# Cross-attention queries computed features-first, with their rms factor applied in the exponential and pools that wait by tile

## The chip, the cores and the metric

The kernel runs on one core of a Trainium2 chip. The metric is the device time of one execution in microseconds (us), the lower the better. Engines are named as in the profile: PE is TensorE (matmuls and transposes), DVE is VectorE, ACT is ScalarE, POOL is GpSimd, and SP is the engine that issues the DMA transfers here. Each engine takes its instructions in the order in which they stand in its own program; it waits in that order for semaphores of the others.

## The reference

One layer of an encoder, on 1024 tokens of 1024 features in float32. Three steps, each added to its input:

```
h = x + W_out [ FoX(xn) ++ GLA(xn) ]                      xn = rms_norm(x)
h = h + CrossAttn(rms_norm(h), rms_norm(mem))
y = h + W2 relu(W1 rms_norm(h))^2
```

The second step is the one that changes:

```
q = rms_norm((hn @ wq).reshape(B, S, 4, 256), q_norm_g)
k, v = jnp.split(memn @ wkv, 2, axis=-1)      # 256 memory tokens
k = rms_norm(k.reshape(B, M, 4, 256), k_norm_g)
s = jnp.einsum('bshd,bmhd->bhsm', q, k) / math.sqrt(256)
p = jax.nn.softmax(s, axis=-1)
o = jnp.einsum('bhsm,bmhd->bshd', p, v).reshape(B, S, D)
return o @ wo
```

So every query is divided by the root of its mean square over the 256 features of its head, before the product with k. The gains of the two norms can be moved into k, and they are. The rms of h itself cancels in the norm of q, save for the epsilon: h enters unnormalised, and the epsilon is scaled by h's mean square (`hev`).

## The kernel before

**Precision and matmuls.** Each float32 operand is split in two parts, a high one (names ending in h: wh, sh, qh, th, oh) and a low one (wl, sl, ql, tl, ol). A product of two such operands is three matmuls for each block of 128 summed features: high·high (L110), and the two mixed ones (L111, L112), all in `gemm`. Splitting is one copy on ACT and one subtraction on DVE (`evac_split`, L117 and L118; for weights L99 and L100 with a gain, L88 and L93 without).

**Stages.** `mixer_inputs` and `fox` compute the first step's two kinds of attention up to 559 us. `project_out` (559 to 592 us) multiplies with W_out: for each half of 512 tokens and each of eight blocks of 128 features it takes 12 or 6 matmuls, loads a partial sum hr from memory (L851, three buffers), adds both into h (L856), squares the block on ACT (L169, sqT, three buffers) and sums the squares on POOL (L170, acc). At the end of a half, `token_squares` turns the sums by four transposes into mean squares for each token (hv, hev, hr of `consts`). h stands in SBUF features-first: 128 features in the partitions, 1024 tokens along the row. `xattn` is the second step (592 us to about 750), `project_o_first` and `project_o_rest` its output projection, and `mlp` (from 840 us to the end) the third.

**xattn before.** There are eight units: two pairs of heads (n) by four groups of 256 tokens (u). `queries` takes each of a unit's two token tiles (128 tokens): `split_tile` splits h of this tile over all 1024 features (ACT L819, DVE L820, 128x1024 each), 24 matmuls of 128x512 give the queries of two heads tokens-first, `head_rstd` forms the factor r for each token and head (a Square on ACT, L144; a reduction on DVE, L146; small operations on POOL), DVE multiplies by r (L995), four transposes turn the result features-first (L998), and it is split. `attend` takes a unit's queries: per token tile 12 matmuls of 128x256 for the scores, the negative maximum (L1014), two Exps with the maximum as bias (L1020), POOL scales p by the reciprocal sum (L1024), four transposes (L1027) and a split; then the products with v over 256 tokens (128x256 matmuls), whose split results o go to memory (od, L1038). The projection loads them again as oh and ol (`load_o`), when all heads of a half are stored.

**What sets the order.** The code gives each engine's work in one sequence; a scheduler then orders each engine's program by its own model of the times, keeping to the dependencies. Memory is handed out by pools on two stacks, left and right, of one address range: a pool opened where another was closed gets its memory, and its first users wait for the former users. All loads and stores of this stage stand on one queue of SP.

## Time and profile before

| | us |
|---|---|
| time, median of 3 runs | 1452.56 (1452.08 to 1454.16) |
| the profiled execution | 1454.34 |
| its span | 1452.6 |
| 560 to 720 us: PE busy | 160.00 of 160.00 |
| 720 to 760 us: PE busy | 38.73 of 40.00 |
| 820 to 840 us: PE busy | 18.69 of 20.00 |

The span is what the profiler's records cover; the rest of the execution's time, 1.74 us, lies around it. "Busy" adds up the time in which an engine works on an instruction; a PE instruction's length includes its way through the array, so that matmuls overlap, and the distance of two starts tells what one costs. In the rows of the trace, the text in brackets is the idle time just ahead of the instruction and what ended it. "PEclk" or the column behind the engines' busy times is the granted clock of TensorE, 1.00 at full speed.

### The profile page before, as it was taken

Reading aid. Unit: us, or ns where it says so; the run is one execution under the profiler, and the core shown is the slowest. Engines: PE = TensorE matmul, PEld = TensorE weight load, DVE = VectorE, ACT = ScalarE, POOL = GpSimd, SP = SyncE. Lnnn points to the kernel's source line nnn. Section 1 sums busy time; section 2 is a strip of 40 time slices with the busy share of each in tenths; the row PEclk is TensorE's granted clock in tenths of the full one; section 3 lists DMA queues with packets and bytes.
Section 4 is the critical chain, followed back from the end, with each engine's and each line's share of the span. In section 5 each row is a group of like instructions: output and inputs, shape, how many; then the busy total and the mean of one; then the engine's idle time right before and its main releaser. Section 6 shows DMA issues by size and latency. Waiting matters only on the chain.

```text
span 1452.6 us, 19224 instructions
## 1 busy us (share of the span) xinstructions
PE 1427.7 (98%) x7068; PEld 1190.0 (82%) x7068; DVE 948.6 (65%) x1354; ACT 679.9 (47%) x1095; POOL 397.1 (27%) x404
## 2 busy tenths in 40 slices
PE   9999999998999999999999999999999999999998
PEld 7788788887888887888888878887888888888887
DVE  5366732428798776666644895636556968788796
ACT  4444341327678565455542364445546735335230
POOL 3235513312242223521212300000000542333454
PEclk9999999999999999999999999999999999999999
DMA  8435520268677642412474124444445835336353
GB/s 273 128 73 131 138 70 1 73 176 252 203 211 234 188 140 87 132 59 88 150 266 170 51 80 153 174 174 189 174 174 209 322 121 188 131 122 225 119 198 119
DMA packets 121166, 223.94 MB, mean 154 GB/s; under 512 B 8912, under 2 KB 54512, under 8 KB 118512
## 3 DMA queue, kind: packets, MB, share of 16 engines
q1 hardware_dynamic: 119776, 218.25, 46.5%
q10 hardware_dynamic: 1296, 4.46, 1.0%
q8 instruction: 56, 0.92, 0.3%
q14 instruction: 38, 0.31, 0.1%
HBM read 150.59 MB, written 72.09 MB: 153 GB/s over the span
## 4 chain that ended last, share of the span: by engine, by line
PE 71%; issue 16%; DMA 6%; DVE 3%; ACT 2%; POOL 1%; ACTq 0%; SPq 0%; DVEq 0%; POOLq 0%
PE mm L110 13%; PE mm L112 13%; PE mm L111 13%; PE my L111 5%; PE my L112 5%; PE my L110 5%; PE tr L111 2%; PE tr L112 2%; PE tr L110 2%; PE tr L696 2%; PE pv L703 1%; DMA xt<-in_x_dram 1%; DMA raw<-in_w_in_dram 1%; PE pv L704 1%; PE s L656 1%
## 5 line engine op out<-in xcount | busy, mean ns | idle before, releaser
L111 PE MATMUL my<-x,g 128*128 128x512 f32 x464 | 180.6, 389 | 1.3 <-DVE x L1076 1.3
L110 PE MATMUL my<-x,g 128*128 128x512 f32 x464 | 180.6, 390 | 0.4 <-ACT h L1281 0.4
L112 PE MATMUL my<-x,g 128*128 128x512 f32 x464 | 180.5, 389 | 0.0
L111 PE MATMUL mm<-wl,xh 128*128 128x512 f32 x320 | 126.5, 396 | 0.9 <-DVE wl L100 0.8
L110 PE MATMUL mm<-wh,xh 128*128 128x512 f32 x320 | 126.0, 397 | 1.0 <-DVE sq L307 1.0
L112 PE MATMUL mm<-wh,xl 128*128 128x512 f32 x320 | 125.9, 394 | 0.0
L1075 ACT ACTIVATE g<-s 128x1024 fp32r<-128x1024 f32 (+1 forms) x72 | 68.7, 962 | 105.0 <-PE my L112 39.1
L1076 DVE TENSOR_TENSOR g<-raw,g 128x512 fp32r<-128x512 f32 (+3 forms) x72 | 69.2, 964 | 67.6 <-ACT g L1075 67.4
L111 PEld LDWEIGHTS my<-x,g 128*128 128x128 f32 x464 | 87.1, 188 | 19.9 <-DVE x L1076 1.7
L1101 POOL TENSOR_TENSOR s<-raw 128x384 f32<-128x384 f32 (+1 forms) x20 | 25.8, 1291 | 282.7 <-DVE h L1196 213.8
L110 PEld LDWEIGHTS my<-x,g 128*128 128x128 f32 x464 | 87.1, 188 | 18.8 <-ACT h L1281 0.8
L1075 ACT ACTIVATE g<-raw 128x512 fp32r<-128x512 f32 (+3 forms) x72 | 55.5, 773 | 100.3 <-DMA raw<-in_mlp_w_dram 40.1
L112 PEld LDWEIGHTS my<-x,g 128*128 128x128 f32 x464 | 87.1, 188 | 17.9
L667 POOL TENSOR_SCALAR p<-p,rrec 128x128 f32<-128x128 f32 (+3 forms) x64 | 57.9, 907 | 159.2 <-DVE rrec L666 151.9
L1076 DVE TENSOR_TENSOR g<-s,g 128x1024 fp32r<-128x1024 f32 (+1 forms) x72 | 88.2, 1228 | 7.6 <-ACT g L1075 7.5
L1243 DVE TENSOR_TENSOR x<-x 128x1024 fp32r<-128x1024 f32 (+1 forms) x64 | 76.8, 1220 | 17.3 <-ACT x L1242 17.1
L110 PE MATMUL mm<-x,g 128*128 128x512 f32 x220 | 85.8, 390 | 0.0
L112 PE MATMUL mm<-x,g 128*128 128x512 f32 x220 | 85.7, 389 | 0.0
L111 PE MATMUL mm<-x,g 128*128 128x512 f32 x220 | 85.6, 389 | 0.0
L110 PE MATMUL tr<-x,g 128*128 128x512 f32 x212 | 82.5, 389 | 0.0
L111 PE MATMUL tr<-x,g 128*128 128x512 f32 x212 | 82.5, 389 | 0.0
L112 PE MATMUL tr<-x,g 128*128 128x512 f32 x212 | 82.5, 389 | 0.0
(318 smaller groups left out, 3739.2 us busy)
## 6 DMA issues: line engine op xcount, KB each, us to landing
ud<-h SPq DMA_DIRECT2D x32, 768.0 KB, 3.8
x<-ud SPq DMA_DIRECT2D x48, 512.0 KB, 5.3
raw<-in_mlp_w_dram SPq DMA_DIRECT2D x20, 1024.0 KB, 7.4
raw<-in_mlp_w_dram SPq DMA_DIRECT2D x16, 768.0 KB, 6.0
raw<-in_w_in_dram SPq DMA_DIRECT2D x23, 512.0 KB, 5.0
raw<-in_xattn_wkv_dram SPq DMA_DIRECT2D x16, 512.0 KB, 7.4
od<-o SPq DMA_DIRECT2D x32, 256.0 KB, 4.0
ud<-h SPq DMA_DIRECT2D x32, 256.0 KB, 2.8
```

The lines of the kernel that those rows point to most:

```text
L110: mm(ps, lh[k], rh[k], start=start and k == 0, stop=False, **kw)
L111: mm(ps, lh[k], rl[k], start=False, stop=False, **kw)
L112: mm(ps, ll[k], rh[k], start=False, stop=stop and k == n - 1, **kw)
L656: nc.tensor.matmul(ps[:, c], qa[:, ts], ka[:, c], start=True, stop=False)
L667: nc.gpsimd.tensor_scalar(p[:, 0:n], p[:, 0:n], rr, 1.0, ALU.mult, ALU.mult)
L696: nc.tensor.transpose(o, pp[i][:, kb * P:(kb + 1) * P], self.ident)
L703: nc.tensor.matmul(pv, va[:, kb, :], th[:, js], start=kb == 0, stop=False)
L704: nc.tensor.matmul(pv, va[:, kb, :], tl[:, js], start=False, stop=kb == nb - 1)
L1075: self.nc.scalar.activation(hi, src, AF.Copy)
L1076: self.nc.vector.tensor_tensor(lo, src, f(hi), ALU.subtract)
L1101: eng.tensor_tensor(s[:, 0], raw[:, 3], raw[:, 2], ALU.add)
L1243: nc.vector.tensor_tensor(lo, f(lo), f(hi), ALU.subtract)
```

## The change

Three edits in one.

*Queries features-first.* The units are now four: a pair of heads (n) by a half of 512 tokens. `query` multiplies the other way round, the weights' 128 columns by 512 tokens, so that the queries come out features-first and are split at once, unnormalised. h is split by feature blocks of 128x512 (`split`), each serving all of a unit's four `query` calls. Each result is also squared on ACT (sq, L989); POOL adds the two squares of a head (L993), four transposes turn the sum tokens-first (L996), and a reduction and three small POOL operations give r, a factor for each token and head. r enters as the `scale` of the Exp, and the negative maximum is multiplied by r ahead of it. `scores` works per tile of 128 tokens as before, `values` on 512 tokens at once, and each od store carries both parts of 512 tokens.

*Pools that wait by tile.* The pools of xattn and of the output projection, which follow on others' memory, are opened with `reuse_waits="tile"`: a tile's first user waits for the former users of its own bytes, where it waited for those of the whole pool. Their sizes change: six buffers of queries, 12 pairs of split blocks of h, one buffer of k and v.

*Squares of h's second half.* Its sum has memory of its own (`acc1`), and `h1_factors(1)`, once the end of `project_out`, is called behind the second query.

The core of the diff (unchanged parts of the scores, the outer loop's `keep` and the pools of `project_o_rest` are left out):

```diff
-            self.acc = [self.T(xp, [P, 512], F32, f"acc{i}", bufs=1) for i in range(2)]
+            self.acc = [self.T(xp, [P, 512], F32, "acc", bufs=1), self.acc1]
...
+                if half == 0:
+                    self.h1_factors(half)
...
-                    A = self.split_tile(sp, (self.h[:, :, t * P:(t + 1) * P],))
-                    ps = self.T(mmp, [P, 512], F32, "mm")
-                    self.gemm(ps, *A, *Ws[n])
-                    qn = self.T(qnp, [P, 512], F32, "qn")
-                    r = self.head_rstd(ps, qn, 2, self.hev[:, t:t + 1])
-                    nc.vector.tensor_tensor(v2(qn), v2(ps), self.bcast(r, 256), ALU.mult)
-                    tp = self.T(trp, [P, 512], F32, "tr")
-                    for j in range(4):
-                        nc.tensor.transpose(tp[:, j * P:(j + 1) * P], qn[:, j * P:(j + 1) * P], self.ident)
-                    self.evac_split(qh[:, i], ql[:, i], v4(tp))
...
+            sp = self.open(sst, "sp", 12, side="right", **kw)
+            def split(half, ks):
+                out = []
+                for k in ks:
+                    sh = self.T(sp, [P, 512], F32R, "sh")
+                    sl = self.T(sp, [P, 512], F32R, "sl")
+                    self.evac_split(sh, sl, self.h[:, k, half * 512:(half + 1) * 512])
+                    out.append((sh, sl))
+                return out
+            def query(u, W, A, j):
+                ps = self.T(mmp, [P, 512], F32, "mm")
+                c = slice(j * P, (j + 1) * P)
+                self.gemm(ps, *([w[:, c] for w in w_] for w_ in W), *zip(*A))
+                q = self.T(qp, [P, 2, 512], F32R, "q")
+                self.evac_split(q[:, 0], q[:, 1], ps)
+                Q.setdefault(u, []).append(q)
+                sq = self.T(sqp, [P, 512], F32, "sq")
+                nc.scalar.activation(sq, ps, AF.Square)
+                if j % 2 == 0:
+                    self.sq0 = sq
+                    return
+                nc.gpsimd.tensor_tensor(sq, sq, self.sq0, ALU.add)
+                tp = self.T(trp, [P, 512], F32, "tr")
+                for t in range(4):
+                    nc.tensor.transpose(tp[:, t * P:(t + 1) * P], sq[:, t * P:(t + 1) * P], self.ident)
+                ss = self.T(self.smallp, [P, 4], F32, "ss4")
+                nc.vector.tensor_reduce(ss, v4(tp), AX.X, ALU.add)
+                nc.gpsimd.tensor_scalar(ss, ss, 1.0 / 256, None, ALU.mult)
...
+                nc.gpsimd.tensor_tensor(ss, ss, self.hev[:, 4 * half:4 * half + 4], ALU.add)
...
+                nc.gpsimd.tensor_tensor(R[u][:, j // 2, :], ss, self.mhalf[:, 0:4], ALU.pow)
...
+                nc.vector.tensor_tensor(nm, nm, r, ALU.mult)
...
-                        nc.scalar.activation(p[:, c], ps[:, c], AF.Exp, bias=nm[:, h:h + 1], accum_out=rs[:, h:h + 1])
+                    nc.scalar.activation(p[:, c], ps[:, c], AF.Exp, bias=nm[:, h:h + 1], scale=r[:, h:h + 1], accum_out=rs[:, h:h + 1])
...
+            def values(u):
+                for j in range(4):
+                    pv = self.T(pvp, [P, 512], F32, "pv")
+                    self.gemm(pv, *([vm[:, i, m, c] for m in range(2)] for i in range(2)),
+                              [th[:, m] for m in ms], [tl[:, m] for m in ms])
+                    o = self.T(pp, [P, 2, 512], F32R, "o")
+                    self.evac_split(o[:, 0], o[:, 1], pv)
+                    nc.sync.dma_start(self.od[:, :, half, 4 * n + j, :], f(o))
...
+            units = [(0, 0), (0, 1), (1, 1), (1, 0)]
...
             sst.close()
-            attend(*units[-1], q[-1])
-            self.project_o_first()
+            self.ost, self.O = ExitStack(), {}
+            self.load_o(self.open(self.ost, "op0", side="right", **kw), 1)
+            self.Wo = self.wsplit(self.wo[:, 0:512], None)
+            for t in range(4):
+                scores(3, t)
+            for i in range(4):
+                if i == 2:
+                    values(3)
+                self.o_block(self.Wo, 0, 1, i, self.T(self.mmp, [P, 512], F32, "mm"))
```

Two places in the engines' orders follow. The names carry a running number, which is not the same before and after; a row gives line, operation, output, inputs and shape.

The first place is the passage from `project_out` to the queries, on ACT. Before, the first two token tiles (sh, 128x1024) are split right behind the squares of the first half's blocks, the other tiles later:

```order
L169 ACTIVATE sqT_5983<-h_5805 128x512
L819 ACTIVATE sh_6226<-h_5805 128x1024
L819 ACTIVATE sh_6271<-h_5805 128x1024
L166 ACTIVATE acc_1376_5813<-h_5805 128x512
L169 ACTIVATE sqT_6045<-h_5805 128x512
L99 ACTIVATE wh_6196<-raw_6190,cols_74 128x512
```

and the last squares of the second half stand there, with the third tile behind them:

```order
L169 ACTIVATE sqT_6109<-h_5805 128x512
L99 ACTIVATE wh_6216<-raw_6210,cols_74 128x512
L99 ACTIVATE wh_6888<-raw_6886,cols_74 128x512
L169 ACTIVATE sqT_6122<-h_5805 128x512
L169 ACTIVATE sqT_6135<-h_5805 128x512
L819 ACTIVATE sh_6318<-h_5805 128x1024
```

Now the first split of all stands behind the last square (the wh rows are the queries' weights):

```order
L169 ACTIVATE sqT_6099<-h_5805 128x512
L169 ACTIVATE sqT_6112<-h_5805 128x512
L99 ACTIVATE wh_6206<-raw_6200,cols_74 128x512
L99 ACTIVATE wh_6746<-raw_6744,cols_74 128x512
L169 ACTIVATE sqT_6125<-h_5805 128x512
L169 ACTIVATE sqT_6138<-h_5805 128x512
L117 ACTIVATE sh_6214<-h_5805 128x512
L117 ACTIVATE sh_6218<-h_5805 128x512
```

What was ahead of the second half's squares, the first operands of the queries, is now behind them. On DVE the low parts stand in the same way behind the last additions into h (L843) and two weights' low parts:

```order
L843 TENSOR_TENSOR h_5805<-mm_6104,hr_6102 128x512
L843 TENSOR_TENSOR h_5805<-mm_6117,hr_6115 128x512
L843 TENSOR_TENSOR h_5805<-mm_6130,hr_6128 128x512
L100 SCALAR_TENSOR_TENSOR wl_6207<-raw_6200,cols_74,wh_6206 128x512
L100 SCALAR_TENSOR_TENSOR wl_6747<-raw_6744,cols_74,wh_6746 128x512
L118 TENSOR_TENSOR sl_6215<-h_5805,sh_6214 128x512
L118 TENSOR_TENSOR sl_6219<-h_5805,sh_6218 128x512
```

The second place is the end of the queries, on ACT. Before, the conversions g of the MLP's first weights stand among the queries of the second pair of heads:

```order
L1020 ACTIVATE p_7230,rs_1687_7231<-s_7215,nm_1685_7228 128x256 x2
L117 ACTIVATE o_7097<-pv_7084 128x512
L117 ACTIVATE o_7115<-pv_7102 128x512
L1020 ACTIVATE p_7260,rs_1693_7261<-s_7245,nm_1691_7258 128x256 x2
L1075 ACTIVATE g_1882_8379<-raw_1881_8377 128x512
L117 ACTIVATE qh_7121<-tr_7206 128x512
L117 ACTIVATE th_7213<-tr_7238 128x512
L819 ACTIVATE sh_7503<-h_5805 128x1024
L144 ACTIVATE qn_7342<-mm_7317 128x512
L1075 ACTIVATE g_1884_8384<-raw_1883_8382 128x512
```

Now they stand among the last unit's work, ahead of the Exps of its last two tiles (p, the rows of L1026; o is an output of `values`, th the transposed p):

```order
L117 ACTIVATE o_7379<-pv_7372 128x512
L88 ACTIVATE wh_7824<-raw_7822 128x512
L117 ACTIVATE o_7390<-pv_7383 128x512
L1026 ACTIVATE p_7518,rs_1747_7519<-s_7502,nm_1745_7515,rq_7267 128x256 x2
L1026 ACTIVATE p_7549,rs_1753_7550<-s_7533,nm_1751_7546,rq_7267 128x256 x2
L1106 ACTIVATE g_1845_8202<-raw_1844_8200 128x512
L1106 ACTIVATE g_1847_8207<-raw_1846_8205 128x512
L117 ACTIVATE th_7500<-tr_7526 128x4x128
L1026 ACTIVATE p_7580,rs_1759_7581<-s_7564,nm_1757_7577,rq_7267 128x256 x2
L117 ACTIVATE th_7500<-tr_7557 128x4x128
L117 ACTIVATE o_7401<-pv_7394 128x512
L1026 ACTIVATE p_7611,rs_1765_7612<-s_7595,nm_1763_7608,rq_7267 128x256 x2
```

On SP, the loads of these weights moved with them, to a place behind the first four loads of oh and ol and ahead of the stores od of the third unit:

```order
L80 DMA raw_7480<-in_xattn_wo_dram 128x2x512
L80 DMA raw_7490<-in_xattn_wo_dram 128x2x512
L861 DMA oh_7450<-od_64 128x1024
L862 DMA ol_7451<-od_64 128x1024
L861 DMA oh_7450<-od_64 128x1024
L862 DMA ol_7451<-od_64 128x1024
L80 DMA raw_7822<-in_xattn_wo_dram 128x2x512
L1127 DMA raw_1844_8200<-in_mlp_w_dram 128x2048
L1127 DMA raw_1846_8205<-in_mlp_w_dram 128x2048
L80 DMA raw_7832<-in_xattn_wo_dram 128x2x512
L1047 DMA od_64<-o_7368 256x1x512
L1047 DMA od_64<-o_7379 256x1x512
```

Before, they stood ahead of all oh and ol, among the stores of the fourth unit and ahead of those of the fifth:

```order
L1038 DMA od_64<-o_7097 128x2x256
L1096 DMA raw_1881_8377<-in_mlp_w_dram 128x2048
L1038 DMA od_64<-o_7097 128x2x256
L1038 DMA od_64<-o_7115 128x2x256 x2
L1096 DMA raw_1883_8382<-in_mlp_w_dram 128x2048
L1038 DMA od_64<-o_7288 128x2x256
L1038 DMA od_64<-o_7306 128x2x256
L1038 DMA od_64<-o_7288 128x2x256
L1038 DMA od_64<-o_7306 128x2x256
L80 DMA raw_7823<-in_xattn_wo_dram 128x2x512
L80 DMA raw_7833<-in_xattn_wo_dram 128x2x512
L868 DMA oh_7793<-od_64 128x1024
```

More of the change, by code (lines that the diff above doesn't have):

```diff
@@ L910, in project_o_rest @@
             self.ost.close()
-            self.acc = [self.T(p, [P, 512], F32, "acc") for p in (self.open(mx, "acc", side="right"), xp)]
+            self.acc = [self.acc1, self.T(xp, [P, 512], F32, "acc")]
             x0 = self.open(mx, "x0", 2, side="right", **kw)
@@ L1041, in xattn @@
-            units = [(0, u) for u in range(4)] + [(1, u) for u in (2, 3, 0, 1)]
-            q = []
-            for i, (n, u) in enumerate(units):
-                if i % 4 == 0:
-                    weights(n)
-                q.append(queries(n, u))
-                if i >= 1:
-                    attend(*units[i - 1], q[i - 1])
-                if i == 4:
-                    kst.close()
-            sst.close()
-            attend(*units[-1], q[-1])
-            self.project_o_first()
+            def split(half, ks):
[6 more added lines that the diff above has]
+                return out
@@ new lines, in scores @@
+            def scores(u, t):
+                kT = KV[units[u][0]][0]
+                ts = slice(t * P, (t + 1) * P)
+                if t == 0:
+                    TH[u] = [self.T(ptp, [P, 4, 512], F32R, n) for n in ("th", "tl")]
+                ps = self.T(sps, [P, 512], F32, "s")
+                for h in range(2):
+                    ks = (2 * h, 2 * h + 1)
+                    self.gemm(ps[:, h * M:(h + 1) * M], *([Q[u][k][:, i, ts] for k in ks] for i in range(2)),
+                              *([kT[:, i, k, :] for k in ks] for i in range(2)))
+                r = R[u][:, :, t]
+                nm = self.T(self.smallp, [P, 2], F32, "nm2")
+                nc.vector.tensor_reduce(nm, v2(ps), AX.X, ALU.max, negate=True)
+                nc.vector.tensor_tensor(nm, nm, r, ALU.mult)
+                p = self.T(pp, [P, 512], F32, "p")
+                rs = self.T(self.smallp, [P, 2], F32, "rs2")
+                rr = self.T(self.smallp, [P, 2], F32, "rr2")
+                for h in range(2):
+                    c = slice(h * M, (h + 1) * M)
+                    nc.scalar.activation(p[:, c], ps[:, c], AF.Exp, bias=nm[:, h:h + 1], scale=r[:, h:h + 1], accum_out=rs[:, h:h + 1])
+                nc.vector.reciprocal(rr, rs)
+                for h in range(2):
+                    c = slice(h * M, (h + 1) * M)
+                    nc.gpsimd.tensor_scalar(p[:, c], p[:, c], rr[:, h:h + 1], 1.0, ALU.mult, ALU.mult)
+                tp = self.T(trp, [P, 512], F32, "tr")
+                for j in range(4):
+                    nc.tensor.transpose(tp[:, j * P:(j + 1) * P], p[:, j * P:(j + 1) * P], self.ident)
+                self.evac_split(*(v[:, :, ts] for v in TH[u]), v4(tp))
@@ new lines, in values @@
+            def values(u):
+                n, half = units[u]
+                vm = KV[n][1]
+                th, tl = TH[u]
+                for j in range(4):
+                    pv = self.T(pvp, [P, 512], F32, "pv")
+                    c, ms = slice(j * P, (j + 1) * P), (2 * (j // 2), 2 * (j // 2) + 1)
+                    self.gemm(pv, *([vm[:, i, m, c] for m in range(2)] for i in range(2)),
[3 more added lines that the diff above has]
+                    nc.sync.dma_start(self.od[:, :, half, 4 * n + j, :], f(o))
@@ new lines, in xattn @@
+            units = [(0, 0), (0, 1), (1, 1), (1, 0)]
+            A = []
+            for u, (n, half) in enumerate(units):
+                if u % 2 == 0:
+                    W = self.wsplit(self.wq[:, n * 512:(n + 1) * 512], C_XAT)
+                if u == 0:
+                    memory(0)
+                    A = split(half, range(KT))
+                keep = A
+                for j in range(4):
+                    if j == 3 and u in (0, 2):
+                        A = split(units[u + 1][1], range(4))
+                    query(u, W, keep, j)
+                    if u == 0 and j == 1:
+                        self.h1_factors(1)
+                    if u and j < 2:
+                        scores(u - 1, 2 * j)
+                        scores(u - 1, 2 * j + 1)
+                    elif u and j == 2:
+                        values(u - 1)
+                        if u == 2:
+                            memory(1)
+                if u in (0, 2):
+                    A = A + split(units[u + 1][1], range(4, KT))
```

108 lines of the change are left out of this document (26 added, 82 removed).

## The prediction

> **What bounds the kernel now.** I read the page's busy totals first, then the windows of the changed stages, then who waited for whom on PE.
>
> ```profile
> PE 1427.7 (98%) x7068; PEld 1190.0 (82%) x7068; DVE 948.6 (65%) x1354; ACT 679.9 (47%) x1095; POOL 397.1 (27%) x404
> ```
>
> PE stands still for only 1452.6 − 1427.7 = 24.9 us of the span. The windows (length, then PE, PEld, DVE, ACT and POOL busy, the granted clock, DMA share, GB/s) show where the changed stages stand:
>
> ```profile
> 580.00:600.00 20.00, 20.00 (x92) 16.54 (x91) 15.60 (x19) 10.24 (x17) 14.45 (x12) 1.00 0.48 143
> 640.00:660.00 20.00, 20.00 (x134) 18.23 (x132) 16.23 (x26) 14.59 (x28) 4.12 (x8) 1.00 0.44 146
> 700.00:720.00 20.00, 20.00 (x121) 17.67 (x120) 13.38 (x22) 10.95 (x23) 4.55 (x10) 1.00 0.25 90
> 720.00:740.00 20.00, 19.56 (x128) 17.34 (x127) 12.24 (x23) 10.42 (x26) 4.76 (x9) 1.00 0.83 274
> 740.00:760.00 20.00, 19.17 (x117) 16.96 (x116) 8.37 (x17) 7.46 (x16) 2.23 (x3) 1.00 0.66 229
> ```
>
> From 580 to 720 PE is never idle; from 720 to 760 it loses 0.44 + 0.83 = 1.27 us, and its longest wait there is for the attention output coming back from memory:
>
> ```profile
> PE mm L110 <- DMA oh<-od: 0.8, 1, 0.8
> ```
>
> So the stage is PE-bound. Work taken from DVE, ACT or POOL buys nothing here; PE work taken away counts in full, and every new PE wait counts in full against it.
>
> **PE work removed.** Pitches first (start, length, row):
>
> ```profile
> 592.16 0.39 PE L110 MATMUL mm<-wh,sh 128*128 128x512 f32 x1
> ...
> 596.92 0.39 PE L110 MATMUL mm<-wh,sh 128*128 128x512 f32 x1
> ```
>
> Between these two lie 21 matmuls: 4.76 / 21 = 0.2267 us for 128x512. A group of four transposes, a 128x256 matmul, and two counts (the last rows are groups of equal instructions from 592 to 760: busy time, mean ns, idle time before):
>
> ```profile
> 703.34 0.40 PE L111 MATMUL mm<-wl,sh 128*128 128x512 f32 x1
> 703.58 0.60 PE L1027 MATMUL tr<-ident,p 128*128 128x128 f32 x4
> 703.93 0.48 PE L112 MATMUL mm<-wh,sl 128*128 128x512 f32 x1
> 704.25 0.40 PE L110 MATMUL mm<-wh,sh 128*128 128x512 f32 x1
> 690.39 0.28 PE L112 MATMUL pv<-th,vm 128*128 128x256 f32 x1
> 690.51 0.28 PE L111 MATMUL pv<-tl,vm 128*128 128x256 f32 x1
> ...
> L110 PE MATMUL pv<-th,vm 128*128 128x256 f32 x64 | 17.0, 286 | 0.0
> L998 PE MATMUL tr<-ident,qn 128*128 128x128 f32 x64 | 10.1, 272 | 0.0
> ```
>
> From 703.34 to 704.25 are 0.91 us for two matmuls and the group, so the group costs 0.91 − 2 × 0.2267 = 0.46 us. The 16 groups on the queries go (L998, 64 single transposes), 8 groups on the sums of squares come: −8 × 0.46 = **−3.7 us**. The products with v are 192 matmuls (64 in each of the three rows of which one is shown) at 0.12 = 23.0 us before and 96 at 0.2267 = 21.8 us after: **−1.2 us**. Query products, score products and the transposes of p keep count and shape. Sum **−4.9 us**, nearly certain, since it is only counting.
>
> The rest lies on engines with room.
>
> ```profile
> L170 POOL TENSOR_TENSOR acc<-acc,sqT x28: 1284/1300/3222, 571.8 to 834.6; 128x512 f32<-128x512 f32 x28
> ```
>
> ACT loses 16 splits of 1024 columns and gets 24 of 512, so a quarter less; POOL gets 8 additions like this row's, with a median of 1.30 us: 10.4 us spread over 130 us, beside the 4 to 5 busy in 20 above. DVE loses a multiplication of 512 columns for each of 16 token tiles. The new multiplication of the maximum by r is a 128x2 operation on DVE, which has 4 to 7 us free in each window. I cost all of this at nothing while the queries run, since the 24 matmuls of a query (24 × 0.2267 = 5.4 us) cover one round of it; without that cover a round would cost up to POOL's 1.30. At the two ends of the stage the cover is missing, and there I look below. That the squares of h's second half are summed up beside the queries moves nothing on PE: its four transposes stood among the query matmuls before, too.
>
> **The start of the queries: a new stall.** Before, the first two token tiles are split long ahead:
>
> ```profile
> 591.94 0.39 PE L112 MATMUL mm<-sh,wl 128*128 128x512 f32 x1
> ...
> 578.46 1.99 ACT L819 ACTIVATE sh<-h 128x1024 fp32r<-128x1024 f32 x2
> 579.60 3.71 DVE L820 TENSOR_TENSOR sl<-h,sh 128x1024 fp32r<-128x1024 f32 x2 [0.63 <-ACT sh L819]
> ```
>
> so PE passes from the last matmul of the output projection (591.94) to the first of the queries (592.16, above) without a gap. Now a query needs h features-first: 512 tokens of it, split in a pool of 24 tiles that lies on memory the output projection gives back, its hr and sqT tiles among it. In the order of the changed kernel the first split stands on ACT behind every square of the second half, and it waits for the last hr loads besides. When that point is reached, the trace of before tells:
>
> ```profile
> 590.17 0.94 SPq L851 DMA_DIRECT2D hr<-hpd  x2
> 589.46 1.27 DVE L856 TENSOR_TENSOR h<-mm,hr 128x512 f32<-128x512 f32 x2
> 594.90 1.34 DVE L856 TENSOR_TENSOR h<-mm,hr 128x512 f32<-128x512 f32 x2 [2.10 <-DMA hr<-hpd]
> 596.15 2.44 DVE L100 SCALAR_TENSOR_TENSOR wl<-raw,cols,wh 128x512 fp32r<-128x512 f32 x2
> 595.68 1.28 ACT L169 ACTIVATE sqT<-h 128x512 f32<-128x512 f32 x2 [0.72 <-DVE h L856]
> ```
>
> The two last hr loads are issued when the two additions at 589.46 free their buffers, land at 594.9, and the last two squares end at 595.68 + 1.28 = 596.96. Taken over unchanged: first split on ACT to 597.6, its low part on DVE behind the two wl (to 598.6), done at 599.3; that low part is an operand of PE's third matmul, due at 592.6 if PE ran on, so PE is 6.7 us late. Against that: the two early low parts (3.71 us at 579.6) are gone from DVE, so the additions and with them the hr loads can come up to 1.3 us sooner, and without POOL beside it a wl takes 0.75 us (its row at 591.45), not 1.22:
>
> ```profile
> 591.45 0.75 DVE L100 SCALAR_TENSOR_TENSOR wl<-raw,cols,wh 128x512 fp32r<-128x512 f32 x1
> ```
>
> With loads landing at 593.2 the last addition ends at 594.0, the two wl at 595.5, the low part at 596.2: 3.6 us late. Range 3.6 to 6.7, I take **+5.2 us**, the middle, since the additions wait partly for PE. Behind it PE needs 6 matmuls (1.36 us) for each pair of splits (0.64 on DVE, half of the 1.27 above), so no further stall.
>
> **The granted clock.** The trace shows what idle stretches do:
>
> ```profile
> 334.37 0.40 PE L111 MATMUL mm<-sl,wh 128*128 128x512 f32 x1
> 336.30 0.79 PE L112 MATMUL mm<-sh,wl 128*128 128x512 f32 x1 [1.53 <-DVE wl L93]
> 332.00:338.00 6.00, 4.04 (x14) 2.58 (x13) 6.00 (x12) 4.34 (x10) 2.48 (x2) 0.78 1.08 381
> 338.00:344.00 6.00, 5.55 (x25) 4.49 (x25) 6.00 (x12) 4.26 (x10) 2.26 (x1) 0.65 1.04 340
> 535.00:545.00 10.00, 8.85 (x52) 7.55 (x53) 8.38 (x20) 7.08 (x18) 3.09 (x5) 0.83 0.25 78
> 545.00:560.00 15.00, 12.50 (x95) 11.05 (x94) 12.80 (x23) 11.39 (x23) 2.88 (x4) 1.00 0.00 1
> ```
>
> The clock falls to half for (0.22 + 0.35) × 6 / 0.5 = 6.8 us, and for 0.17 × 10 / 0.5 = 3.4 us, each time among short idles like that of 1.53; in the last row PE idles 2.5 us in pieces and keeps its clock. A gap of 4 to 6 us is worse. Half rate for 3.4 us costs 1.7 us of PE time, for 6.8 us 3.4. Range 0 to 3.4, I take **+1.7 us**.
>
> The Trainium skill (TensorE: Matmul & The Clock Gate, Part 1, the HAM clock gate) says that the clock falls after a fully idle window of about 3.4 us, in windows that run free of the kernel. By that rule a gap of 5.2 us holds such a window about half the time, and in the other half the clock stays up and the sum is 1.7 us less. The rows above speak against it, since the clock fell there without any idle of that length; it stands among the rivals.
>
> **The end of the stage.** Before, ACT and DVE work on the last token tiles while PE still has queries of others. Now the last query matmul completes the last head of four token tiles at once: its square, POOL's addition (1.30), the transposes, a reduction, three small POOL operations, then for each tile a maximum, the Exp pairs and POOL's scaling, all in a chain behind the last query matmul; PE has in its order, until the last transposes of p, 48 scores, 48 matmuls of 512 columns and three groups of transposes: 48 × 0.12 + 48 × 0.2267 + 3 × 0.46 = 18.0 us.
>
> ```profile
> 692.02 0.35 SPq L1096 DMA_DIRECT2D raw<-in_mlp_w_dram  x1
> 698.20 0.63 ACT L1075 ACTIVATE g<-raw 128x512 fp32r<-128x512 f32 x1 [3.08 <-DMA raw<-in_mlp_w_dram]
> SPq L868 <- DMA od<-o: 6.7, 4, 4.5
> DMA packets 5809, 10.06 MB, mean 239 GB/s; under 512 B 416, under 2 KB 3488, under 8 KB 5807
> ```
>
> The two 1-MB loads of the MLP's weights stood before at 692 and two later, in a quiet stretch; ACT waited 3.08 us for one, and PE didn't notice. Now they stand on SP's queue behind the first oh and ol loads, which can only go when the last query matmul has freed their memory, and their two conversions (g) stand on ACT ahead of the last two tiles' Exps. From the last query on 4.5 MB have to land (2 of oh and ol, 0.5 of weights, these 2): at the 239 GB/s of 718 to 760 (the last line) 19 us, at half as much again 13 us, against PE's 18. The od stores of these heads queue behind the same bytes, and oh loads wait for them (4.5 us at longest before). I count 4 us of PE idle (2, if the bytes land in 13 us and only the chain shows; 7, if 19 us, the conversion, an Exp pair, the scaling and a turn through od come in series), less the 1.27 that goes: **+2.7 us** (0.7 to 5.7).
>
> **Sum.** −4.9 + 5.2 + 1.7 + 2.7 = **+4.7 us**. Against the profiled execution (1454.34: span 1452.6 and 1.74 around it) 1459.0; that one ran 1.78 over the median of 1452.56, so against the median **1457.3**. All low ends give −4.9 + 3.6 + 0 + 0.7 = −0.6, all high ends −4.9 + 6.7 + 3.4 + 5.7 = +10.9: 1452 to 1463.5.
>
> **The rivals.**
>
> *The stalls are hidden (faster).* If the last hr loads land before 590, ACT and DVE reach the first split while PE is still in the output projection. This decides from new waits of less than 4.9 − 2.9 = 2.0 us in all. For it: DVE is 4.4 us less busy than PE in 580 to 600. Against it: three hr buffers, so that these loads go only after the additions to blocks that PE ends at 592.3 − 4 × 1.36 = 586.9 and one later, and they take 594.9 − 590.2 = 4.7 us. It gives −4.9 + about 1 = 1448.6. Chance 0.13.
>
> *The clock stays up.* The gap falls so that nothing lowers the clock, as in 545 to 560; all else as forecast: −4.9 + 5.2 + 2.7 = +3.0, so 1455.6. Chance 0.12. (By the rule of the Trainium skill quoted above, from TensorE: Matmul & The Clock Gate, it would be about as likely as the forecast.) The trace gives it less: a drop followed two of the three clusters of idle above.
>
> *The start stalls, but nothing else.* The clock stays up and the tail costs what it did: −4.9 + 3.6 to 5.2 = −1.3 to +0.3, so 1451 to 1453. Chance 0.13.
>
> *The tail becomes the bound.* Loads land at the slow rate, and the last oh pair waits for od stores that stand behind two MB of weights: the turn of 4.5 us plus a load of 4.7 in series, beyond the 7 us above by 3 or more: +8 to +13, 1461 to 1466. For it: the DMA share of 0.83 in 720 to 740 even without the two MB. Against it: PE has four of eight k-steps and two units' products to do meanwhile. Chance 0.15.
>
> That the change doesn't take the PE work away is no case: its count and shapes stand in the order.
>
> **How the numbers follow.** My forecast (three new costs, 1454 to 1460) 0.47, and the rivals 0.13, 0.12, 0.13 and 0.15. Range 1448.5 to 1465, which leaves half of the fast rival and the tip of the slow one out. Differences under 0.2% (2.9 us) can't be told from none here. Faster than 1449.7: the first rival, 0.13. Within: the third rival, half of the second, which lies at the bound, and the low end of the forecast, 0.13 + 0.06 + 0.08 = 0.27. Slower than 1455.5: 0.60.
>
> **What would show it.** Right: a PE gap of 3.6 to 6.7 us at about 592 that ends with sh or sl, the granted clock at 0.5 just behind it, transposes only on sums of squares and on p, some us of idle before the last transposes of p or the first oh of a later k. Wrong: no gap at 592 (then the order of additions and loads was read wrongly), a clock of 1.00 behind the gap, or idle in the middle of the queries, where I costed ACT, DVE and POOL at nothing.

## The result, and the profile after

| | before | after |
|---|---|---|
| time, median (runs) | 1452.49 us (4; 1452.08 to 1454.16) | 1472.54 us (4; 1468.95 to 1474.39) |
| span of the profiled execution | 1452.6 | 1472.7 |
| first matmul of the MLP (my<-x,g) starts at | 832.04 | 842.05 |
| from there to the last matmul of the MLP | 615.49 | 625.52 |

After stands to before as 1.0133 (95% interval 1.0112 to 1.0154): 20 us slower, 7.5 us above the top of the predicted range. The span grew by 20.1 us, and the table splits it into two equal halves: 10.0 us up to the first matmul of the MLP, and 10.0 us inside the MLP, of which the change touches no line.

The page's busy total of PE, after:

```profile
PE 1439.5 (98%) x6940; PEld 1183.5 (80%) x6940; DVE 939.6 (64%) x1354; ACT 680.7 (46%) x1103; POOL 399.1 (27%) x404
```

PE has 128 instructions fewer (7068 before), just as counted: 64 transposes of qn go and 32 of sq come, 192 products with v go and 96 come. Yet its busy time has grown by 11.8 us, and only 33.2 us of the span are not busy. Some of the work that stayed has become dearer, and the lowered clock seen below is only a part of it.

The waits of PE from 560 to 900 us, after (what PE waited for, us in total, times, the longest):

```profile
PE mm L110 <- ACT sh L117: 4.2, 1, 4.2
PE tr L1033 <- POOL p L1030: 2.7, 2, 1.6
PE mm L111 <- DVE sl L118: 2.0, 1, 2.0
```

The new waits are those that the prediction named: sh and sl at the start, p at the end. The windows of after (length, PE, PEld, DVE, ACT, POOL busy, granted clock, DMA share, GB/s):

```profile
590.00:600.00 10.00, 3.77 (x14) 2.48 (x13) 8.01 (x12) 8.46 (x16) 7.41 (x5) 0.85 0.42 145
600.00:610.00 10.00, 10.00 (x38) 8.01 (x37) 5.56 (x11) 2.36 (x5) 0.00 (x0) 0.81 0.01 2
640.00:660.00 20.00, 20.00 (x113) 17.26 (x112) 11.24 (x20) 11.54 (x25) 6.00 (x9) 1.00 0.25 82
745.00:755.00 10.00, 7.26 (x35) 5.65 (x35) 5.31 (x14) 4.85 (x13) 1.88 (x4) 0.83 0.68 228
```

At the start PE loses 6.23 us and then runs at a lowered clock; in the middle of the queries it is never idle; at the end it loses 2.74 us, and the clock falls again. But in a stretch of the MLP where PE has no idle time and a clock of 1.00, the same 100 us hold 443 matmuls before and 434 after. First before, then after:

```profile
1200.00:1300.00 100.00, 100.00 (x443) 82.80 (x442) 79.65 (x96) 43.68 (x55) 29.00 (x24) 1.00 0.47 156
```

```profile
1200.00:1300.00 100.00, 100.00 (x434) 81.22 (x433) 76.63 (x86) 48.22 (x60) 28.98 (x24) 1.00 0.53 178
```

That is 2% fewer, and no idle time or clock explains it. The timeline of PE shows where it is: twelve matmuls of the MLP, from start to start, before,

```profile
943.14 0.39 PE L111 MATMUL mm<-x,g 128*128 128x512 f32 x1
...
945.86 0.39 PE L111 MATMUL mm<-x,g 128*128 128x512 f32 x1
```

and the very same twelve (the 482nd to the 493rd of the MLP; the second row of each pair is the one behind them) after:

```profile
954.54 0.39 PE L111 MATMUL mm<-x,g 128*128 128x512 f32 x1
...
957.34 0.39 PE L111 MATMUL mm<-x,g 128*128 128x512 f32 x1
```

2.72 / 12 = 226.7 ns before, 2.80 / 12 = 233.3 ns after: same line, shape and type, 6.6 ns more for each. It isn't so for all. Forty microseconds later after's matmuls go at the old pitch again, 2.72 us for twelve:

```profile
995.29 0.39 PE L111 MATMUL my<-x,g 128*128 128x512 f32 x1
...
998.01 0.39 PE L111 MATMUL my<-x,g 128*128 128x512 f32 x1
```

Over the 2688 matmuls of the MLP (distances above 245 ns, which are waits or changes of shape, left out) the mean distance is 226.74 ns before, with 98% at 226 or 227, and 230.70 ns after, with 33%. 2687 × 3.96 ns = 10.6 us: that is the second half of the loss; of the 0.6 us that it is too much, 0.4 is one wait that the slower PE no longer meets.

**What differs between the two dozens.** The compiled programs' memory addresses tell. The new tile rq (128 partitions, 2 × 4 floats, 32 bytes in each partition) is allotted in the pool of small tiles, which keeps six buffers of a kind: 6 × 32 = 192 bytes. That pool is opened near the kernel's beginning, at the bottom of the stack of pools on the memory's left side, and so all that lies above it on that side moves up by 192 bytes, for the rest of the kernel: an x7 of the MLP from 9184 to 9376, a g2 from 91104 to 91296. Pools opened on the right side stay, so that the other x7 is at 161760 and a g1 at 141280 in both programs. In the dozen at 954 us, x (33952 for its first) lies on the left and g (122848) on the right; at 995, both (40096 and 94880) lie on the left and have moved together. Taken modulo 256, the addresses of moving tile and weight tile agree in all 2688 matmuls of the MLP before, and after in 1344 of them; in 1056 they are 192 apart and in 288 they are 64 apart. The mean distance is 233.3 ns where the moving tile's address less the weight tile's is 192 modulo 256, 231.4 where it is 64, and 228.5 where the two agree: behind a change from one kind to another, the distance takes some matmuls to settle (past the first 30 of a stretch, those that agree are back at 227.1). These three classes make up the 10.6 us. The theory for the experiments: **a matmul costs 226.7 ns when its moving tile and its weight tile lie at addresses that agree modulo 256, and more, up to 233.3, when they don't; the change brought its left and right tiles out of step.** The rival: the other order of the instructions is to blame (other neighbours on PE, other traffic of ACT, DVE and DMA during the MLP).

### The profile page after: what moved, and what is told of

Same layout as the page of the kernel before. It is cut to its first block, busy times and chain, and to the rows that moved or that the text cites. A ratio compares the mean times of both kernels' runs of the same rounds, so it can differ in the third digit from the quotient of the medians.

```text
span 1472.7 us, 18914 instructions
## 1 busy us (share of the span) xinstructions
PE 1439.5 (98%) x6940; PEld 1183.5 (80%) x6940; DVE 939.6 (64%) x1354; ACT 680.7 (46%) x1103; POOL 399.1 (27%) x404
## 4 chain that ended last, share of the span: by engine, by line
PE 86%; DMA 6%; DVE 4%; ACT 2%; issue 1%; POOL 0%; SPq 0%; DVEq 0%; ACTq 0%; POOLq 0%
PE mm L111 14%; PE mm L110 14%; PE mm L112 14%; PE my L111 7%; PE my L112 7%; PE my L110 7%; PE tr L110 3%; PE tr L112 3%; PE tr L111 3%; PE tr L697 1%; DMA raw<-in_w_in_dram 1%; DMA xt<-in_x_dram 1%; PE pv L704 1%; PE pv L705 1%; PE s L657 1%
## 5 line engine op out<-in xcount | busy, mean ns | idle before, releaser
L110 PE MATMUL my<-x,g 128*128 128x512 f32 x464 | 182.5, 394 | 0.0
L110 PE MATMUL mm<-wh,xh 128*128 128x512 f32 x320 | 126.0, 397 | 0.0
L110 PE MATMUL mm<-sh,wh 128*128 128x512 f32 x256 | 102.5, 402 | 4.8 <-ACT sh L117 4.2
L111 PE MATMUL mm<-sl,wh 128*128 128x512 f32 x256 | 102.0, 399 | 2.0 <-DVE sl L118 2.0
L112 PE MATMUL mm<-sh,wl 128*128 128x512 f32 x256 | 102.3, 400 | 1.6 <-DVE wl L93 1.6
L112 PEld LDWEIGHTS my<-x,g 128*128 128x128 f32 x464 | 87.1, 188 | 20.1
L110 PEld LDWEIGHTS my<-x,g 128*128 128x128 f32 x464 | 87.1, 188 | 20.0 <-ACT h L1312 0.3
L110 PE MATMUL mm<-x,g 128*128 128x512 f32 x220 | 86.5, 393 | 0.0
```

What stands on the lines that cost most here:

```text
L110: mm(ps, lh[k], rh[k], start=start and k == 0, stop=False, **kw)
L111: mm(ps, lh[k], rl[k], start=False, stop=False, **kw)
L112: mm(ps, ll[k], rh[k], start=False, stop=stop and k == n - 1, **kw)
```

## The experiments

**1. The new tile in a pool of its own** (after, with this edit), which is opened last in the cross-attention and closed with it. The engines' orders are those of after; what lies behind the pool of small tiles goes back to its address of before.

```diff
+            rqp = self.open(st, "rq4", 6, **kw)
...
-                    R[u] = self.T(self.smallp, [P, 2, 4], F32, "rq")
+                    R[u] = self.T(rqp, [P, 2, 4], F32, "rq")
```

> The factors r (six buffers of 32 bytes) get a pool of their own at the end of the attention's pools, so that every other tile on the left stack lies 192 bytes lower, at its address of before; the order of all instructions is that of the changed kernel. Theory (alignment): matmuls that read one operand from the left stack and one from the right slow each other down when the two are not a multiple of 1024 bytes apart. Then the MLP's 2688 matmuls fall back from 230.7 to 226.7 ns, 10.7 us, and the queries and the output projection gain some 2 to 3 more: 1458 to 1461. PE's gap of 6.2 us at the start of the queries stays. Rival (the slower matmuls follow from the state in which the gap or the clock leaves PE): nothing changes, 1470 to 1474.

Measured: 1465.05 us (1460.67 to 1465.63), 1.0068 of before (1.0045 to 1.0091), span 1463.9. The same MLP window, in this kernel:

```profile
1200.00:1300.00 100.00, 100.00 (x443) 82.81 (x442) 81.79 (x93) 48.34 (x60) 32.35 (x26) 1.00 0.53 176
```

443 matmuls again, at a mean distance of 226.75 ns, with ACT's and DMA's busy time still that of after (48.3 and 0.53, not 43.7 and 0.47). So the pitch goes with the addresses, not with the order or the traffic. The time fell by 7.5 us, less than the 10.6 of the pitch, and misses the expected band (1458 to 1461) by 4 us. The trace shows why. PE, around 1169 us, and on ACT the instruction it waits for:

```profile
1169.55 0.50 PE L110 MATMUL my<-x,g 128*128 128x512 f32 x1 [2.54 <-ACT h L1313]
```

```profile
1168.90 1.09 ACT L1313 ACTIVATE h<-my 128x512 f32<-128x512 f32 x2 [1.80 <-DMA ud<-h]
```

A faster PE meets a wait there (on stores ud that free memory) which the slower one of after didn't; here 2.54 us are followed by 3.4 us at half clock, 1.7 us lost. The pitch alone doesn't make this wait: before, at the same pitch, has 0.36 us at this place, while the other changed kernels at the old pitch (those of 4 with 10 buffers, 5 and 6) have 1.1 to 2.2. So the changed order of the instructions has a part in it; which part, no run here tells. The stall at the start stays as in after:

```profile
596.13 0.73 PE L110 MATMUL mm<-sh,wh 128*128 128x512 f32 x2 [4.18 <-ACT sh L117]
```

**2. The 192 bytes alone** (before, with this edit): nothing is computed otherwise, and every engine's order is that of before.

```diff
             self.smallp = self.open(st, "small", 6)
+            self.T(self.open(st, "pad"), [P, 48], F32, "pad")
```

> The kernel before with 192 bytes of unused memory behind its pool of small tiles, so that the left stack moves up as the change moves it; the order of all instructions stays. Theory (alignment): the MLP's matmuls take about 231 ns instead of 226.7, the time rises by 10 to 16 us to 1463 to 1468, with no new wait on PE. Rival (state after the gap): nothing changes, 1452 to 1454.

Measured: 1464.21 us (1462.91 to 1464.82), 1.0071 of before (1.0056 to 1.0086), span 1461.2. The MLP window:

```profile
1200.00:1300.00 100.00, 100.00 (x434) 81.21 (x433) 80.95 (x94) 45.48 (x58) 29.82 (x25) 1.00 0.47 157
```

434 matmuls and a mean distance of 230.70 ns, both those of after. An unused tile of 192 bytes makes the kernel of before 11.6 us slower, as expected (1463 to 1468). In the profiled executions the MLP takes 9.9 us more and the work of the stage ahead of it 2.2; their spans differ by only 8.6, since the one of before had 10.2 us at half clock on its way and this one none until its end. In its queries hardly any matmul keeps the old pitch; twelve of them, L110 to L110:

```profile
601.19 0.39 PE L110 MATMUL mm<-wh,sh 128*128 128x512 f32 x1
...
603.99 0.39 PE L110 MATMUL mm<-wh,sh 128*128 128x512 f32 x1
```

2.80 / 12 = 233.3 ns. The theory holds, and the rival falls.

**3. Other amounts.** Is it any shift at all, or its remainder? The same edit with [P, 32], [P, 64] and [P, 128] makes pads of 128, 256 and 512 bytes.

> The kernel before with its left stack 128 bytes higher; the order of all instructions stays. Known: at a shift of 0 the MLP's matmuls take 226.7 ns, at 192 bytes 230.7. If the two operands only have to agree modulo 128 or 64 bytes, 226.7 here; if modulo 256 or more, about 230 to 231 and a span 9 to 12 us over the 1452 of before.

> The kernel before with its left stack 256 bytes higher. If the operands have to agree modulo 256 bytes, 226.7 ns and some 1452 us; if modulo 512 or 1024, about 230 to 231 ns and 9 to 12 us more.

> The kernel before with its left stack 512 bytes higher, the length of one row of a 128x128 weight tile. If the operands have to agree modulo 512 bytes or less, 226.7 ns and some 1452 us; if modulo 1024, about 230 to 231 ns and 9 to 12 us more.

One run each, beside 1451.10 for before on the same chip: 1461.03 for 128 bytes, 1451.45 for 256, 1450.61 for 512. The mean distance over the MLP's matmuls is 230.38, 226.73 and 226.73 ns. The MLP window with 128, then with 256, then with 512 bytes:

```profile
1200.00:1300.00 100.00, 100.00 (x435) 81.44 (x434) 81.10 (x94) 44.25 (x56) 29.01 (x25) 1.00 0.47 156
```

```profile
1200.00:1300.00 100.00, 100.00 (x443) 82.82 (x442) 80.00 (x95) 43.32 (x54) 30.86 (x26) 1.00 0.46 154
```

```profile
1200.00:1300.00 100.00, 100.00 (x443) 82.80 (x442) 79.97 (x97) 43.04 (x54) 31.67 (x26) 1.00 0.45 151
```

128 and 192 bytes cost 10 to 12 us, 256 and 512 nothing: the remainder modulo 256 decides. With 128 bytes the matmuls whose tiles don't agree take 232.4 ns, a little less than the 233.3 at 192. (A shift of less than 128 bytes was not run; a difference of 64 occurs in after, above.)

**4. The start: memory for the splits.** In after the first split of h waits for memory: the pool sp of the splits (12 buffers each for sh and sl) lies on the hr and sqT tiles of the output projection. With fewer buffers it reaches less far. Experiment 1 with 10 buffers, and after with 9:

```diff
-            sp = self.open(sst, "sp", 12, side="right", **kw)
+            sp = self.open(sst, "sp", 10, side="right", **kw)
```

> As the first run, and the pool of h's split blocks has 10 pairs of buffers instead of 12, so that its memory ends above that of the output projection's hr and sqT tiles: the first split waits for no load. In the order the first splits now stand among the squares of h's first half. Theory (start of the queries): the gap of 6.2 us at 592 and the half clock behind it (3.4 us) go; with the alignment too 1472.5 - 13.3 - 6.2 - 3.4 = 1449.6, so 1448 to 1452, at or below the time before. Rival (the gap comes from the squares' and additions' own lateness, not from the shared memory): the gap stays, 1458 to 1461.

> The changed kernel with 9 pairs of split blocks instead of 12, which frees them of the memory of hr and sqT without moving anything on the left stack. Theory: the gap at 592 and the half clock behind it go, the slow matmuls stay: 1472.5 - 6.2 - 3.4 = 1463, so 1461 to 1465. If the slow matmuls were a consequence of the gap or of the clock, they would go too and the time would be 1449 to 1453.

With 10: 1456.78 us (1451.32 to 1457.95), 1.0020 of before (1.0006 to 1.0034), span 1452.4. The stall and the clock behind it, in this kernel:

```profile
591.50 0.50 PE L110 MATMUL mm<-sh,wh 128*128 128x512 f32 x1 [1.63 <-DVE h L843]
600.00:610.00 10.00, 10.00 (x49) 8.42 (x48) 0.76 (x3) 2.39 (x4) 1.88 (x2) 1.00 0.08 30
```

6.2 us of idle have become 1.63 and the clock stays at 1.00, and the time is about 8 us less than in experiment 1, some 7 of them at the start by the two traces: the start stall was a matter of the memory under sp. That it did not reach the expected 1448 to 1452 has two reasons. One is the 1.63 us that are left, a wait for the last additions into h, and DVE's rows suggest where they come from:

```profile
572.58 0.68 DVE L843 TENSOR_TENSOR h<-mm,hr 128x512 f32<-128x512 f32 x1
573.18 6.28 DVE L118 TENSOR_TENSOR sl<-h,sh 128x512 fp32r<-128x512 f32 x4
579.39 0.68 DVE L843 TENSOR_TENSOR h<-mm,hr 128x512 f32<-128x512 f32 x1
579.99 0.68 DVE L118 TENSOR_TENSOR sl<-h,sh 128x512 fp32r<-128x512 f32 x1
```

```profile
569.43 9.49 POOL L170 TENSOR_TENSOR acc<-acc,sqT 128x512 f32<-128x512 f32 x6 [18.70 <-ACT sqT L169]
```

The splits now stand on DVE ahead of the additions into h, and while POOL sums up squares (569.43 to 578.92) one takes 6.28 / 4 = 1.57 us, against 0.68 behind it. The addition at 572.58, one of whose inputs is a PSUM tile, takes 0.68 in the midst of POOL's work. The Trainium skill (SBUF — State Buffer, Who interferes with whom) says that an instruction of DVE with two inputs in SBUF gets in the way of GpSimd instructions that read SBUF, and one with a single such input doesn't; these rows agree with both parts. That the slow splits are what makes the last additions late is argued from the rows; no run shows it alone. The other reason is the end of the stage, which is as it was:

```profile
735.86 0.28 PE L112 MATMUL s<-kT,q 128*128 128x256 f32 x1
...
738.00 0.89 PE L1034 MATMUL tr<-ident,p 128*128 128x128 f32 x4 [1.63 <-POOL p L1031]
739.96 1.14 PE L1034 MATMUL tr<-ident,p 128*128 128x128 f32 x4 [1.07 <-POOL p L1031]
735.00:745.00 10.00, 7.28 (x39) 5.86 (x38) 5.84 (x15) 4.85 (x14) 1.86 (x4) 0.83 0.68 231
```

After with 9 buffers, and rq left in its place: 1465.77 us (1463.03 to 1469.3), 1.0084 (1.0063 to 1.0106). That is 0.8 us above the expected band. The stall shrinks to 0.95 us and the MLP's distance stays at 230.72 ns. The two faults are independent.

**5. The end of the stage.** Which wait ends last there? Two edits to the kernel of 4 with 10 buffers. The first gives the scores three PSUM buffers and the products with v one:

```diff
-            sps = self.open(st, "s4", 2, space=PSUM, **kw)
-            pvp = self.open(st, "pv4", 2, space=PSUM, **kw)
+            sps = self.open(st, "s4", 3, space=PSUM, **kw)
+            pvp = self.open(st, "pv4", 1, space=PSUM, **kw)
```

> The third run's kernel with three PSUM buffers for scores and one for the products with v, instead of two and two. Theory (end of the stage): the idle of 1.6 + 1.1 us before the last transposes of p comes from scores that wait for a buffer until the order has nothing else left; now 18 products with v and 12 matmuls of the projection stand between the last scores and these transposes (6.8 us against a chain of some 4), the idle goes and the half clock behind it too: some 4 us less than the 1452.4 of that run's span. Rival: with one buffer every product with v waits for the copy of the one before (some 1 us each), and 3 to 8 us come instead.

Measured: 1474.47 us in one run, far slower, and by more than the rival's 3 to 8 us. The longest waits of PE:

```profile
PE pv L110 <- DVE o L118: 4.2, 2, 2.8
PE mm L110 <- DMA oh<-od: 3.2, 2, 2.5
PE mm L110 <- ACT wh L88: 2.8, 1, 2.8
```

Products now wait until the one before is split, and the loads of the attention output are waited for longer. Whether a third buffer for the scores alone would bring anything, this run doesn't tell. The second edit moves the memory of the MLP's raw weights: the pool raw7 is opened ahead of the pool x0, and so lies elsewhere and comes free later.

```diff
+            self.raw7 = self.open(mx, "raw7", 2, side="right", **kw)
             x0 = self.open(mx, "x0", 2, side="right", **kw)
...
-            self.raw7 = self.open(mx, "raw7", 2, side="right", **kw)
```

> The third run's kernel, with the memory of the MLP's raw weights taken ahead of that of its first operands, so that it lies on oh and ol of the first projection half and not on h's split blocks: the two 1-MB loads and their conversions leave the end of the queries and come behind the projection's first half. Theory (end of the stage): the conversions delay the last two tiles' chain, the loads delay od, oh and ol. The idle before the last transposes of p (1.6 + 1.1 us) shrinks to 1 us or less, the half clock behind it (1.7 us) goes: 3 to 4 us less than that run, 1452 to 1454 and thus no slower than before. Rival: the loads are then late for the MLP, which starts with a wait of 2 us or more: no gain or a loss.

Measured: 1454.31 us (1450.13 to 1456.3), 1.0001 of before (0.9990 to 1.0013), 0.3 us above the expected band. The first loads of these weights now go at 788 us. Waits from 560 to 860, and the window that had a clock of 0.83:

```profile
PE mm L111 <- DMA ol<-od: 1.4, 2, 0.8
PE mm L110 <- DMA oh<-od: 0.8, 2, 0.4
PE pv L110 <- ACT th L117: 0.7, 1, 0.7
735.00:745.00 10.00, 8.05 (x54) 6.64 (x52) 4.65 (x11) 5.17 (x15) 3.18 (x7) 1.00 0.74 223
```

The two waits for p are gone, with the half clock behind them. In their place stand waits for oh, ol and th, 10 − 8.05 = 1.95 us in this window. But the conversions g and their loads are not all that left the place: the order of PE changed with them.

```profile
738.16 0.60 PE L1034 MATMUL tr<-ident,p 128*128 128x128 f32 x4
739.13 0.73 PE L110 MATMUL mm<-oh,wh 128*128 128x512 f32 x2 [0.37 <-DMA oh<-od]
...
743.14 1.04 PE L1034 MATMUL tr<-ident,p 128*128 128x128 f32 x8
```

Twelve matmuls of the projection now stand between the last scores and the last transposes of p, 5.1 us from the last score (738.03) to these transposes. In the kernel of 4 no matmul of the projection stood there. From the start of the last score to the first scaled half of its p, the chain takes 3.3 us here and took 4.0 there. So without the conversions the chain is some 0.7 us shorter, and the rest of the 2.7 us is covered by PE's other work; on which of the two the half clock hung is not shown.

**6. Two more parts alone,** each an edit to the kernel of 4 with 10 buffers: the cross-attention's pools wait as before, not tile by tile, and the factors of h1's second half are worked out in the output projection as before.

```diff
-            kw = dict(reuse_waits="tile")
+            kw = {}
```

```diff
-                if half == 0:
-                    self.h1_factors(half)
+                self.h1_factors(half)
...
-                    if u == 0 and j == 1:
-                        self.h1_factors(1)
```

> The third run's kernel with the attention's pools waiting for whole pools, as before the change; the order of all instructions stays. Theory: with ten pairs of split blocks above the shared memory, nothing that matters is left for the finer wait to spare: 1455 to 1459, as the third run (1456.8). Rival (the finer waits are what the change gains by): 3 us or more slower.

> The third run's kernel with h1_factors(1) at the end of the output projection, as before the change. Theory: its four transposes fall among the query matmuls either way, so within 2 us of the third run (1456.8). Rival (the transposes now wait between projection and queries for POOL's last additions): a gap of 2 us or more at 590 to 600, 1459 or more.

Measured: 1455.92 us (1453.85 to 1459.58), 1.0020 (1.0006 to 1.0033), for the first; 1458.46 us (1454.63 to 1461.87), 1.0035 (1.0018 to 1.0051), for the second; the kernel that both started from had 1.0020. So at these sizes of pools the waits by tile are worth nothing that could be measured, and the squares beside the queries at most some 2 us, which the intervals don't tell from nothing.

None of the changed kernels beats before; the best, with all three faults mended (addresses, memory under the splits, weights at the end), is level with it.

## Why the prediction was wrong, point by point

The sum of the prediction was made for the stage ahead of the MLP, so it is compared there: from the matmul at 388.25 us, which is the 1905th of PE and starts at the same time in both traces, to the MLP's first. PE's idle times are summed up from its rows, and of a stretch at half clock half of PE's busy time counts as lost.

| term | predicted | measured, after less before |
|---|---|---|
| PE work | −4.9 | 433.8 − 436.5 = −2.7 |
| stall at the start | +5.2 | 4.20 + 2.03 = +6.2 |
| clock | +1.7 | 5.89 − 1.71 = +4.2 |
| idle at the end, and all other | +2.7 | (14.15 − 6.23) − 5.62 = +2.3 |
| **the stage** | **+4.7** | **+10.0** |
| the MLP | 0 | +10.0 |

**The step that failed: "Query products, score products and the transposes of p keep count and shape",** and with it the silent step that a stage whose lines and order stay costs what it did. Count and shape don't settle the price of a matmul; the addresses of its two operands belong to it. The prediction called the sum of PE's work "nearly certain, since it is only counting", and the counting was right to the instruction (128 fewer). But it priced what stays at nothing, 2688 matmuls of the MLP among it. Experiment 2 shows this step alone: the 192 bytes, with no other change, cost 11.6 us. In after's trace the MLP's part of it is 10.0 of the 20 us: taken off, about 1462 would be left, inside the range. Measured without it, in experiment 1, the time was 1465.05, at the range's very top, because of the wait that came up there. And the stage itself lost 10.0 us, twice the 4.7 of the sum; the terms follow.

**PE work, −4.9:** right in kind, but the saving was smaller. Reckoned in the same way, the kernels with the old addresses (1, 4 with 10 buffers, 5 and 6) need 432.4 to 433.7 us for this stage, so −2.7 to −4.0. In after the slow pitch has a share in it: its query matmuls go at 230.6 ns in the mean, against 228.3 in experiment 1, and half of the projection's at 229.5 against 227.1, together some 1.2 us. Where the rest of the forecast saving went is open.

**The stall at the start, +5.2:** mechanism right, size within the range of 3.6 to 6.7. SP's last two hr loads, DVE's additions and splits, and ACT's squares and splits, after:

```profile
588.84 0.94 SPq L838 DMA_DIRECT2D hr<-hpd  x2
593.46 1.33 DVE L843 TENSOR_TENSOR h<-mm,hr 128x512 f32<-128x512 f32 x2 [1.99 <-DMA hr<-hpd]
594.71 2.42 DVE L100 SCALAR_TENSOR_TENSOR wl<-raw,cols,wh 128x512 fp32r<-128x512 f32 x2
597.05 5.36 DVE L118 TENSOR_TENSOR sl<-h,sh 128x512 fp32r<-128x512 f32 x7
594.24 1.27 ACT L169 ACTIVATE sqT<-h 128x512 f32<-128x512 f32 x2 [0.69 <-DVE h L843]
595.42 4.78 ACT L117 ACTIVATE sh<-h 128x512 fp32r<-128x512 f32 x9
```

The hr loads landed 1.4 us earlier than before, at 593.46, nearly as reckoned for the low end; the two wl still took 1.21 us each (POOL adds up squares beside them from 595.02), where the low end had 0.75. So the first sl began at 597.05 and not at 595.5.

**The clock, +1.7:** too low, and above its range of 0 to 3.4. The gap was followed by the 6.8 us at half rate of the upper bound; PE was busy for 4.9 of them, so 2.5 us were lost. The tail added 1.7, where the prediction had put nothing. The rule of the Trainium skill (TensorE: Matmul & The Clock Gate, Part 1) that a whole idle window of 3.4 us must come first doesn't fit the trace of before: PE idles for only 1.06 of the 3.4 us ahead of the half clock that begins at 335.39. The tail is less clear. In the kernel of 4 with 10 buffers, and again with the pools' waits changed, 3.4 us at half clock begin at about 739.4, in the second of PE's two idle pieces of 1.63 and 1.07 us; idle time and transposes together fill some 3.2 of the 3.4 us ahead. In experiment 1 the same two pieces left the clock at 1.00 (745 to 755 us). So the prediction was right to go by its rows at the gap, and should have reckoned with such a loss, as a chance, for the tail as well.

**The end of the stage, +2.7:** about right, +2.3 (from 718 us to the MLP PE is idle for 3.8 us, where the prediction counted 4 for its end), and in the main by the chain that it gave. ACT, DVE and POOL, after:

```profile
742.07 1.42 ACT L1106 ACTIVATE g<-raw 128x512 fp32r<-128x512 f32 x2
745.18 0.60 ACT L117 ACTIVATE th<-tr 128x512 fp32r<-128x512 f32 x1 [1.70 <-PE tr L1033]
745.68 0.56 ACT L1026 ACTIVATE p<-s,nm,rq 128x256 f32<-128x256 f32 x1
```

```profile
744.57 0.68 DVE L1107 TENSOR_TENSOR g<-raw,g 128x512 fp32r<-128x512 f32 x1
745.16 0.15 DVE L1020 TENSOR_TENSOR nm<-nm,rq 128x2 f32<-128x2 f32 x1
```

```profile
747.34 0.94 POOL L1030 TENSOR_SCALAR p<-p,rr 128x256 f32<-128x256 f32 x2 [3.42 <-DVE nm L1020]
```

The maximum, the Exp and the scaling come in a chain behind the last scores, and PE, with nothing else in its order, waits 1.64 and 1.07 us for p. The MLP's conversion on DVE holds up the small multiplication of the maximum by r until 745.16, but the Exp that needs it starts only at 745.68, behind the split th on ACT, which had waited for PE's transposes. So the conversions, which the prediction put into this chain, are not what ends last in it; in experiment 5, without them, the chain is some 0.7 us shorter, of the 2.7 that PE waits for p here. The loads landed in time: oh and ol cost only 0.47 and 0.55 us, so the rival of the tail as the bound, with its 8 to 13 us, fell.

**ACT, DVE and POOL at nothing in the middle of the queries:** right; PE is not idle at all from 600 to 718 us.

## What to carry to other kernels

Where a change allots even a small tile in a pool that lives long, compare the addresses of the tiles behind it before and after, above all of moving and weight tiles that lie on different stacks; give the tile to a pool that closes with its stage, or pad to a multiple of 256 bytes, which cost nothing here. When a time doesn't add up, take first the distance of two starts in a stage that was not changed: if it moved at an unchanged clock, as here, look at the matmul's operands before looking for waits. And where operands are made ready only just before their use, the price shows at both ends of the stage, where no other work covers the chain: look there for what memory the first tiles lie on, and for what else stands on the engines' queues behind the last.

## What the runs showed of the hardware

A 128x512 matmul with a weight tile of its own took 226.7 ns where the addresses of moving and weight tile agreed modulo 256 bytes. It took more where they didn't, and how much went with the difference, moving less weight: 233.3 ns (2.9% more) at 192, 232.4 at 128, 231.4 at 64, as means over the MLP. Shifting the left-hand tiles by 128 or 192 bytes was slow, by 256 or 512 not. The Trainium skill (TensorE: Matmul & The Clock Gate, Part 2, Step-by-step) says that weights are loaded through a read port apart from that of the moving operand and take nothing from it; by that the addresses of the two shouldn't matter to each other, and the pitch in experiment 2 says they do. Why, whether by banks or by something else, no run here tells.

A gain on PE can uncover a wait elsewhere: in experiment 1 the faster MLP met a wait for stores, 2.54 us, that the slower one of after had passed without.
